# Eight experts taken in the order of their token counts: the three smallest in 64 slots with both halves of the split in one stationary tile, whole-chunk weight splits

## The chip, the cores and the metric

The kernel runs on one core of one Trainium2 chip. The metric is the device time of one execution in microseconds (us). Before the change the median of three runs is 1942.06 us (1941.7 to 1943.23).

## The reference

A trunk of two layers works on 256 tokens of width 1024 in fp32. Each layer has three parallel mixers, a cross-attention and a feed-forward part, each followed by a LayerNorm. The feed-forward part of the first layer is dense; that of the second is a choice of 2 out of 8 experts, and this is the part that the change touches:

```
logits = (x @ w_router).astype(jnp.float32) + b_router.astype(jnp.float32)
top_vals, top_idx = lax.top_k(logits, TOP_K)            # TOP_K = 2
top_w = jax.nn.softmax(top_vals, axis=-1)
combine = jnp.sum(jax.nn.one_hot(top_idx, N_EXPERTS) * top_w[..., None], axis=-2)
out = jnp.zeros_like(x)
for e in range(N_EXPERTS):                              # 8 experts, 1024 -> 2 x 3584 -> 1024
    out = out + combine[..., e:e + 1] * swiglu(x, w_gu[e], w_down[e])
```

With the reference's inputs its routing sends 53, 76, 79, 38, 77, 57, 63 and 69 tokens to experts 0 to 7.

## The kernel before

**Split products.** Every matrix product keeps fp32 accuracy with three products of a shorter type: a tensor w is split into `hi` (ScalarE copies it into the shorter type, `hi_of`) and `lo` (VectorE subtracts, `lo_of`), and a product is hi·hi + hi·lo + lo·hi. Weights arrive in chunks of 128 x 2048 fp32 (1 MB), one DMA each from the SyncE queue, in the order in which they are used. `parts` (line 260) splits a chunk in two halves of 128 x 1024 as they are asked for; the halves of `hi` and of `lo` each live in a ring of three buffers (`wsp`), so that one and a half chunks can stand ready ahead of TensorE. ScalarE writes `whi`, VectorE reads `raw` and `whi` and writes `wlo`, and a chunk's raw buffer is free for the next DMA when VectorE has read its second half.

**Raw buffers.** In the last layer, from the cross-attention on, raw chunks go round a ring of 15 buffers: NFX = 11, one in `xp`, and three in `fifo`.

**The experts (`moe`, line 1170).** After the last LayerNorm the router's logits are turned, VectorE ranks them, and TensorE counts the tokens ahead of each token, which gives each token its slot in each of its two experts (`slot`). `prepare` (1253) builds for a pair of experts a 0/1 matrix `pe` from the slots, gathers by matmul up to 128 tokens per expert (32 matmuls of 256 columns) and copies the result to `xg`, hi and lo apart. Each expert then has 42 chunks. `gate_up` (1292) handles one block of 512 hidden columns: 4 chunks, 48 matmuls of 512 columns with the tokens as the stationary operand (line 1301 hi·hi, 1302 hi·lo, 1303 lo·hi), then SiLU on ScalarE, a product on VectorE, 4 transposes on TensorE (1309), and the split of the result (`hth`, `htl`). `down` (1317) handles 2 chunks, 24 matmuls (lines 450 to 452 of `mm3_x`), one block later than `gate_up`. There are NEB = 7 blocks. `scatter` (1329) splits the sum (`myh`, `myl`), brings it back to token order by 8 matmuls, and adds it to the output with 4 VectorE instructions (line 1340). The experts run in the order 0 to 7. `prepare` stands ahead of expert 0, and at the end of experts 1, 3 and 5 for the next pair.

**More than 128 tokens.** The largest count is read into a register at the end (line 1393); if it is over 128, a loop over all experts does the rest.

**Order.** The order on each engine is made by a scheduler that hoists later work into gaps; the first splits of expert 0's weights thus stand inside the last LayerNorm.

## Time and profile before

| | |
|---|---|
| median of three runs | 1942.06 us |
| the profiled execution: its time | 1947.3 us |
| the profiled execution: span of its core | 1945.4 us |
| mean granted TensorE clock | 0.984 |
| TensorE matmul busy | 1882.1 us (97%) |
| VectorE busy | 1532.6 us (79%) |
| ScalarE busy | 1283.2 us (66%) |
| GpSimd busy | 110.9 us (6%) |
| HBM read | 498.34 MB |

The span runs from the first to the last instruction of the core. Shares of busy time are means over stages that differ: layer 0, the mixer and cross-attention of layer 1 (to about 940 us), and the experts (from there to 1930 us). TensorE's matmuls overlap, and their ends are modelled, so that its busy time is an upper bound of what it does. The groups of the section on the rows are named by number in the prediction.

### The profile page before, as it was taken

Reading aid. Unit: us, or ns where it says so; the run is one execution under the profiler, and the core shown is the slowest. Engines: PE = TensorE matmul, PEld = TensorE weight load, DVE = VectorE, ACT = ScalarE, POOL = GpSimd, SP = SyncE. Lnnn points to the kernel's source line nnn. Section 1 sums busy time; section 2 is a strip of 40 time slices with the busy share of each in tenths; the row PEclk is TensorE's granted clock in tenths of the full one; section 3 lists DMA queues with packets and bytes.
Section 4 is the critical chain, followed back from the end, with each engine's and each line's share of the span. In section 5 each row is a group of like instructions: output and inputs, shape, how many; then the busy total and the mean of one; then the engine's idle time right before and its main releaser. Section 6 shows DMA issues by size and latency. Waiting matters only on the chain.

```text
span 1945.4 us, 27894 instructions
## 1 busy us (share of the span) xinstructions
PE 1882.1 (97%) x10672; PEld 1634.6 (84%) x10672; DVE 1532.6 (79%) x1976; ACT 1283.2 (66%) x1673; POOL 110.9 (6%) x111
## 2 busy tenths in 40 slices
PE   7999999999999999989899999999999999999996
PEld 7998998899989988877688888888888888888875
DVE  7774764794557755755899999999999999999987
ACT  5666554555444555544678787887777778788774
POOL 4030000100004300000200000000000000000000
PEclk9999999999999999989899999999999999999998
DMA  7324553544554343594499998999989999899970
GB/s 255 131 93 153 185 216 134 182 171 163 185 188 170 130 145 121 194 378 173 174 371 371 359 373 320 375 373 355 375 318 375 375 354 374 318 375 368 382 274 24
DMA packets 74924, 503.37 MB, mean 259 GB/s; under 512 B 9504, under 2 KB 11808, under 8 KB 15264
## 3 DMA queue, kind: packets, MB, share of 16 engines
q1 hardware_dynamic: 74496, 500.43, 68.6%
q8 instruction: 85, 1.39, 0.3%
q0 software_dynamic: 144, 1.05, 0.2%
q14 instruction: 55, 0.45, 0.1%
q10 hardware_dynamic: 144, 0.05, 0.0%
HBM read 498.34 MB, written 1.05 MB: 257 GB/s over the span
## 4 chain that ended last, share of the span: by engine, by line
PE 87%; DVE 8%; ACT 3%; issue 2%; DMA 0%; POOL 0%; ACTq 0%; DVEq 0%; POOLq 0%
PE ps L281 8%; PE ps L283 8%; PE ps L282 8%; PE pu L1302 5%; PE dn L450 5%; PE pu L1303 5%; PE pu L1301 5%; PE pg L1303 5%; PE pg L1302 5%; PE dn L451 5%; PE dn L452 5%; PE pg L1301 5%; DVE wlo L221 3%; PE acc L428 2%; PE acc L430 2%; PE acc L432 2%
## 5 line engine op out<-in xcount | busy, mean ns | idle before, releaser
L221 DVE TENSOR_TENSOR wlo<-raw,whi 128x1024 fp32r<-128x1024 f32 x926 | 1118.3, 1229 | 308.4 <-ACT whi L218 295.3
L218 ACT ACTIVATE whi<-raw 128x1024 fp32r<-128x1024 f32 x926 | 974.4, 1060 | 519.3 <-PE ps L282 187.5
L281 PE MATMUL ps<-xhi,whi 128*128 128x256 f32 x992 | 288.3, 291 | 14.8 <-ACT whi L218 14.8
L283 PE MATMUL ps<-xhi,wlo 128*128 128x256 f32 x992 | 286.4, 290 | 4.3 <-DVE wlo L221 4.3
L282 PE MATMUL ps<-xlo,whi 128*128 128x256 f32 x992 | 286.8, 289 | 0.0
L281 PEld LDWEIGHTS ps<-xhi,whi 128*128 128x128 f32 x992 | 194.8, 197 | 16.3 <-ACT whi L218 15.5
L283 PEld LDWEIGHTS ps<-xhi,wlo 128*128 128x128 f32 x992 | 194.8, 197 | 5.8 <-DVE wlo L221 5.1
L282 PEld LDWEIGHTS ps<-xlo,whi 128*128 128x128 f32 x992 | 195.3, 197 | 0.8 <-issue 0.3
L1302 PE MATMUL pu<-wlo,xg 128*128 128x512 f32 x448 | 176.1, 393 | 2.7 <-DVE wlo L221 2.7
L451 PE MATMUL dn<-wlo,hth 128*128 128x512 f32 x448 | 178.0, 400 | 0.1
L1302 PE MATMUL pg<-wlo,xg 128*128 128x512 f32 x448 | 176.6, 394 | 1.4 <-DVE wlo L221 1.4
L1303 PE MATMUL pg<-whi,xg 128*128 128x512 f32 x448 | 175.8, 392 | 0.6 <-DVE xg L1254 0.6
L1301 PE MATMUL pg<-whi,xg 128*128 128x512 f32 x448 | 175.2, 391 | 0.0
L1301 PE MATMUL pu<-whi,xg 128*128 128x512 f32 x448 | 175.1, 391 | 0.0
L1303 PE MATMUL pu<-whi,xg 128*128 128x512 f32 x448 | 174.8, 390 | 0.0
L452 PE MATMUL dn<-whi,htl 128*128 128x512 f32 x448 | 174.0, 391 | 0.0
L450 PE MATMUL dn<-whi,hth 128*128 128x512 f32 x448 | 139.5, 391 | 0.0
L1302 PEld LDWEIGHTS pu<-wlo,xg 128*128 128x128 f32 x448 | 84.1, 188 | 27.6 <-DVE wlo L221 6.6
L1302 PEld LDWEIGHTS pg<-wlo,xg 128*128 128x128 f32 x448 | 84.1, 188 | 24.1 <-DVE wlo L221 3.8
L1301 PEld LDWEIGHTS pu<-whi,xg 128*128 128x128 f32 x448 | 84.1, 188 | 17.9
L450 PEld LDWEIGHTS dn<-whi,hth 128*128 128x128 f32 x448 | 83.9, 188 | 17.8
L1301 PEld LDWEIGHTS pg<-whi,xg 128*128 128x128 f32 x448 | 84.2, 188 | 17.4
(520 smaller groups left out, 2869.5 us busy)
## 6 DMA issues: line engine op xcount, KB each, us to landing
raw<-in_w SPq DMA_DIRECT2D x462, 1024.0 KB, 4.9
lng<-in_ln SPq DMA_DIRECT2D x6, 512.0 KB, 6.4
lnb<-in_ln SPq DMA_DIRECT2D x6, 512.0 KB, 7.2
raw<-in_memt SPq DMA_DIRECT2D x2, 1024.0 KB, 4.7
raw<-in_xt SPq DMA_DIRECT2D x4, 256.0 KB, 5.7
raw<-in_w SPq DMA_DIRECT2D x2, 512.0 KB, 6.0
ux<-us SPq DMA_DIRECT2D x32, 32.0 KB, 2.1
yg<-ux SPq DMA_DIRECT2D x32, 32.0 KB, 1.9
```

The costliest lines, as they stand in the source:

```text
L218: return A.activation(dst, src, AF.Copy, scale=scale)
L221: return V.tensor_sub(dst, src, hi.bitcast(F32))
L281: T.matmul(ps, whi, xhi, start=first, stop=False)
L282: T.matmul(ps, whi, xlo, start=False, stop=False)
L283: return T.matmul(ps, wlo, xhi, start=False, stop=last)
L428: T.matmul(accs[m][n], ah, wh, start=first, stop=False)
L450: T.matmul(ps, ah, wh, start=first, stop=False)
L451: T.matmul(ps, ah, wl, start=False, stop=False)
L452: return T.matmul(ps, al, wh, start=False, stop=last)
L1301: T.matmul(ps, xg[0][:, k, :], wh, start=(k == 0), stop=False)
L1302: T.matmul(ps, xg[0][:, k, :], wl, start=False, stop=False)
L1303: T.matmul(ps, xg[1][:, k, :], wh, start=False, stop=(k == KD - 1))
```

## The change

- **Order by count.** `sort`, on VectorE after the weights of the mixture are known, counts the tokens of experts 1 to 7, ranks them from the largest to the smallest, permutes their slots and weights (`slots`, `combs`), and writes the index of each one's first weight chunk as integers (`firsti`). SyncE reads these seven numbers into registers and takes the weight chunks of experts by register address. Expert 0 runs first as before; then follow, by rank, 0, 4, 1, 5, 2, 6, 3 (`turns`).
- **Three small experts.** Ranks 4, 5 and 6 have 64 slots (HCAP) in place of 128. Their stationary tile holds the hi part in columns 0 to 63 and the lo part in columns 64 to 127, so that two products (with `whi` and with `wlo`) do the work of three: 32 + 16 matmuls per block in place of 48 + 24. The sums of the two halves of the partitions are added behind it: ScalarE copies partitions 64 to 127 of `pg` and `pu` (line 1370), VectorE adds them (1371), then SiLU, product, transposes of 64 partitions, and both splits into one `hth`.
- **Whole-chunk splits.** In the experts `parts` splits a chunk by one ScalarE and one VectorE instruction of 128 x 2048. `hi` goes to a ring of three in `wsp`, `lo` to a new ring of three (`wlo`). Ahead of the experts, halves of `hi` and `lo` share one buffer of `wsp`.
- **Room.** NFX goes from 11 to 8: 12 raw buffers in place of 15.
- **prepare** takes one expert ahead of expert 0, one after the fourth block of expert 0, and pairs at the end of turns 1, 3 and 5: five in place of four.
- The loop for overflow runs if an expert has more tokens than its slots (128, or 64 for the three small ones).

```diff
@@ parts
+            if wide[0]:
+                if not made:
+                    hi = wsp.tile([P, CH], F32R, tag="w", name="whi")
+                    lo = wide[0].tile([P, CH], F32R, name="wlo")
+                    hi_of(hi, raw)
+                    low(lo, raw, hi)
+                    made[0] = hi, lo
+                return [t[:, c0:c1] for t in made[0]]
             h = c0 // HC
             if h not in made:
-                hi = wsp.tile([P, HC], F32R, tag="whi", name="whi")
-                lo = wsp.tile([P, HC], F32R, tag="wlo", name="wlo")
+                both = wsp.tile([P, 2, HC], F32R, tag="w", name="w")
+                hi, lo = both[:, 0], both[:, 1]
...
@@ moe: sort
+                V.tensor_tensor(gt7, others, mine, op=ALU.is_gt)
...
+                V.tensor_reduce(pos7, gt7, axis=AX.X, op=ALU.add)
+                V.tensor_tensor(perm, iota[:, 0:NS].unsqueeze(2).to_broadcast(sh7),
+                                pos7.unsqueeze(1).to_broadcast(sh7), op=ALU.is_equal)
...
+                V.tensor_copy(firsti, first)
...
@@ gate_up
                             T.matmul(ps, xg[0][:, k, :], wh, start=(k == 0), stop=False)
-                            T.matmul(ps, xg[0][:, k, :], wl, start=False, stop=False)
-                            T.matmul(ps, xg[1][:, k, :], wh, start=False, stop=(k == KD - 1))
+                            T.matmul(ps, xg[0][:, k, :], wl, start=False, stop=(few and k == KD - 1))
+                            if not few:
+                                T.matmul(ps, xg[1][:, k, :], wh, start=False, stop=(k == KD - 1))
+                n = HCAP if few else P
...
+                if few:
+                    up = wk.tile([P, 512], F32, tag="htl", name="mup", bufs=2)
+                    for ps, s_ in ((pg, sl), (pu, up)):
+                        A.copy(s_[:n], ps[n:])
+                        V.tensor_add(s_[:n], s_[:n], ps[:n])
+                    A.activation(sl[:n], sl[:n], AF.Silu)
+                    V.tensor_mul(sl[:n], sl[:n], up[:n])
...
@@ the experts
-            for e in range(E):
+            def src(r, off):
+                if r < 0:
+                    return w_in[base + off]
+                if r not in begin:
+                    begin[r] = nc.values_load(firsti[0:1, r:r + 1], engines=[mybir.EngineType.SP], min_val=NCE,
+                                              max_val=NS * NCE)
+                return w_in[ds(begin[r] + (base + off), 1)].rearrange("o p c -> (o p) c")
+
+            turns = [-1, 0, 4, 1, 5, 2, 6, 3]
+            for i, r in enumerate(turns):
...
+                    if i == 0 and nb == 3:
+                        ready += prepare([False], lambda m, j: slots[:, m, turns[1]:turns[1] + 1])
+                if 0 < i < E - 1 and not ready:
+                    rs = turns[i + 1:i + 3]
+                    ready = prepare([q >= NBIG for q in rs], lambda m, j: slots[:, m, rs[j]:rs[j] + 1])
```

The order of the instructions moves at three places. On VectorE, inside the last LayerNorm, before (`bnb` is the shift of the second half of the tokens, `lnx` three of the eight pieces of the normed input to the router):

```order
L238 BN_AGGR bmv<-bst 128x2
L238 TENSOR_SCALAR bve<-bmv 128x1
L238 SCALAR_TENSOR_TENSOR bnb<-bmv,brs 128x1
L221 TENSOR_TENSOR wlo<-raw,whi 128x1024 x3
L238 TENSOR_TENSOR x<-lny,lng 128x1024
L238 TENSOR_SCALAR lnx<-pt,lnt 128x256 x3
L238 TENSOR_TENSOR x<-x,lnb 128x1024
```

and now:

```order
L242 BN_AGGR bmv<-bst 128x2
L242 TENSOR_SCALAR bve<-bmv 128x1
L242 SCALAR_TENSOR_TENSOR bnb<-bmv,brs 128x1
L224 TENSOR_TENSOR wlo<-raw,whi 128x2048 x3
L242 TENSOR_TENSOR x<-lny,lng 128x1024
L242 TENSOR_SCALAR lnx<-pt,lnt 128x256 x3
L242 TENSOR_TENSOR x<-x,lnb 128x1024
```

Three splits stand at the same place, each of a whole chunk in place of a half. On VectorE in the steady part of an expert, before (one block of 6 chunks is the twelve splits from one `htl` to the next):

```order
L221 TENSOR_TENSOR wlo<-raw,whi 128x1024 x6
L1306 TENSOR_TENSOR msl<-msl,pu 128x512
L221 TENSOR_TENSOR wlo<-raw,whi 128x1024 x3
L221 TENSOR_TENSOR htl<-ps,hth 128x512
L221 TENSOR_TENSOR wlo<-raw,whi 128x1024 x9
```

and now one block of a small expert:

```order
L1371 TENSOR_TENSOR msl<-msl,pg 64x512
L224 TENSOR_TENSOR wlo<-raw,whi 128x2048 x2
L1371 TENSOR_TENSOR mup<-mup,pu 64x512
L224 TENSOR_TENSOR wlo<-raw,whi 128x2048
L1373 TENSOR_TENSOR msl<-msl,mup 64x512
L224 TENSOR_TENSOR wlo<-raw,whi 128x2048 x3
L224 TENSOR_TENSOR hth<-ps,hth 128x4x64
```

Twelve splits of halves have become six of whole chunks, and two instructions behind the matmuls four. On the SyncE queue, where the last LayerNorm's loads (`lnb`) are behind it and the experts' chunks follow, before:

```order
L314 DMA lnb<-in_ln 128x1024
L256 DMA raw<-in_w 128x2048 x7
L1393 TENSOR_LOAD cnti
L1393 ISA x2
L256 DMA raw<-in_w 128x2048 x286
```

and now, from the last load of `firsti` on:

```order
L1432 TENSOR_LOAD firsti
L1432 ISA x2
L260 DMA raw<-in_w 128x2048 x2
L1480 TENSOR_LOAD cnti
L1480 ISA x2
L260 DMA raw<-in_w 128x2048 x23
L260 ISA
L260 DMA raw<-in_w 128x2048
```

Seven loads of `firsti` stand in the queue behind those 7 DMAs, with one DMA between the fourth and the fifth, and each chunk taken by register address has one register instruction ahead of it.

## Rows read from the trace of the kernel before

**Rows 1.** Page, part 5: costliest group of TensorE ahead of the experts, with its waits.

```profile
L281 PE MATMUL ps<-xhi,whi 128*128 128x256 f32 x992 | 288.3, 291 | 14.8 <-ACT whi L218 14.8
```

**Rows 2.** Windows: length, PE, PEld, DVE, ACT, POOL busy; clock, DMA share, GB/s.

```profile
830.00:840.00 10.00, 5.45 (x22) 4.86 (x23) 8.36 (x8) 3.06 (x3) 0.00 (x0) 0.54 1.01 427
1200.00:1300.00 100.00, 100.00 (x452) 82.16 (x451) 92.93 (x87) 79.11 (x83) 0.00 (x0) 1.00 0.95 363
```

**Rows 3.** Chain of waits in the experts: start, us, what.

```profile
1070.31 1.40 DVE x L1340 x2
...
1807.30 1.41 DVE x L1340 x2
```

**Rows 4.** Groups by form, 960 to 1910 us: busy us, mean ns of one, idle before.

```profile
L221 DVE TENSOR_TENSOR wlo<-raw,whi 128x1024 fp32r<-128x1024 f32 x653 | 780.8, 1223 | 69.9 <-ACT whi L218 57.9
L218 ACT ACTIVATE whi<-raw 128x1024 fp32r<-128x1024 f32 x651 | 684.5, 1060 | 194.0 <-PE pu L1303 68.0 <-PE pg L1303 67.6 <-PE dn L452 53.6
L221 DVE TENSOR_TENSOR htl<-ps,hth 128x512 fp32r<-128x512 f32 x55 | 37.7, 686 | 1.7 <-ACT hth L218 1.7
L218 ACT ACTIVATE hth<-ps 128x512 fp32r<-128x512 f32 x55 | 32.0, 581 | 4.8 <-PE ps L1309 4.8
L1254 DVE CAST xg<-ps 128x256 fp32r<-128x256 f32 x24 | 10.0, 419 | 0.5 <-PE ps L1273 0.5
```

**Rows 5.** Timeline of VectorE in an expert: start, us.

```profile
1300.91 0.68 DVE L1306 TENSOR_TENSOR msl<-msl,pu 128x512 f32<-128x512 f32 x1
1301.58 3.50 DVE L221 TENSOR_TENSOR wlo<-raw,whi 128x1024 fp32r<-128x1024 f32 x3
...
1312.50 1.28 DVE L221 TENSOR_TENSOR myl<-dn,myh 128x512 fp32r<-128x512 f32 x2
```

**Rows 6.** Chain of waits: steps of TensorE.

```profile
906.72 0.91 PE acc L428 x4
...
1847.92 0.45 PE ps L1309 x4
```

**Rows 7.** Timeline of TensorE at a `prepare` between experts.

```profile
1186.19 0.64 PE L1273 MATMUL ps<-pe,xhi 128*128 128x256 f32 x4
1186.66 0.63 PE L450 MATMUL dn<-whi,hth 128*128 128x512 f32 x2
```

**Rows 8.** Timelines of VectorE, GpSimd and ScalarE in the last LayerNorm.

```profile
925.72 5.64 DVE L221 TENSOR_TENSOR wlo<-raw,whi 128x1024 fp32r<-128x1024 f32 x3
932.42 0.98 DVE L238 TENSOR_SCALAR lnx<-pt,lnt 128x256 f32<-128x256 f32 x2
936.44 0.28 DVE L238 TENSOR_TENSOR cmp<-lg 128x128 f32<-128x128 f32 x1
939.61 0.87 DVE L238 TENSOR_SCALAR pe<-cr,slot 128x128 fp32r<-128x128 f32 x4
...
925.86 3.29 POOL L238 TENSOR_TENSOR x<-x,lnb 128x1024 f32<-128x1024 f32 x1
```

**Rows 9.** Chain of waits: TensorE's first `prepare`.

```profile
940.43 4.39 PE ps L1273 x24
```

**Rows 10.** SyncE: waits, 960 to 1880 us (us, times, longest), and one register load.

```profile
SPq L256 <- DVE wlo L221: 772.5, 309, 4.6
...
L1393 SPq TENSOR_LOAD <-cnti x1: 488/488/488, 957.6 to 957.6; - x1
```

**Rows 11.** Windows of 2 us around falls and rises of the granted clock.

```profile
726.00:728.00 2.00, 2.00 (x12) 2.00 (x11) 1.56 (x2) 0.52 (x2) 0.00 (x0) 0.50 0.03 8
728.00:730.00 2.00, 2.00 (x17) 1.86 (x15) 0.18 (x1) 1.20 (x3) 0.00 (x0) 0.92 0.77 180
...
932.00:934.00 2.00, 1.12 (x5) 0.19 (x4) 1.76 (x4) 0.00 (x0) 0.10 (x1) 1.00 0.93 393
934.00:936.00 2.00, 0.94 (x5) 0.29 (x4) 1.64 (x3) 0.64 (x1) 0.00 (x0) 1.00 0.14 57
936.00:938.00 2.00, 0.16 (x1) 0.16 (x1) 1.84 (x8) 1.36 (x2) 0.00 (x0) 0.63 0.00 0
```

More of the change, by code (lines that the diff above doesn't have):

```diff
@@ L39 @@
 NCE = 42
+HCAP = 64
+NBIG = 4
 ALPHA = (2.0 * L) ** 0.25
@@ L42 @@
 NFIFO = 3
-NFX = 11
+NFX = 8
 LATER = 400
@@ L93, in _constants @@
     e = np.arange(E)
+    put("half", np.tile(i % HCAP, (P, 1)))
     put("lt", np.tile((e[None, :] < e[:, None]).astype(np.float32).reshape(1, 64), (P, 1)))
@@ L227, in tile_trunk @@
     load = [None]
+    wide = [None]
     class Line:
@@ L1243, in weigh, with sort @@
                 V.tensor_add(comb, comb, tmp8)
+                GP.tensor_scalar(x, x, ALPHA, None, op0=ALU.mult)
+            NS = E - 1
+            sh7 = [P, NS, NS]
+            sq = [P, 2, NS, NS]
+            slots, combs, over = t("slots", [P, 2, NS]), t("combs", [P, 2, NS]), t("over", [P, E])
+            capn, firsti = t("capn", [P, E]), mp.tile([P, NS], I32, name="firsti")
+            def sort():
                 ps = pst.tile([P, 512], F32, tag="tr", name="ps")
@@ new lines, in sort @@
+                gt7, eq7 = (old[:, o:o + NS * NS].rearrange("p (e f) -> p e f", e=NS) for o in (0, NS * NS))
+                pos7, perm = t("pos7", [P, NS]), t("perm", sh7)
+                first, most = t("first", [P, NS]), t("most", [P, 1])
+                others = cnt[:, 1:].unsqueeze(1).to_broadcast(sh7)
+                mine = cnt[:, 1:].unsqueeze(2).to_broadcast(sh7)
+                lt7 = ltm[:, 1:, 1:]
+                V.tensor_tensor(gt7, others, mine, op=ALU.is_gt)
+                V.tensor_tensor(eq7, others, mine, op=ALU.is_equal)
@@ new lines, in sort @@
+                V.tensor_copy(firsti, first)
+                both = old2[:, 0:2 * NS * NS].rearrange("p (m e f) -> p m e f", m=2, e=NS)
+                for dst, src in ((slots, slot), (combs, comb)):
+                    V.tensor_mul(both, perm.unsqueeze(1).to_broadcast(sq),
+                                 src[:, :, 1:].unsqueeze(2).to_broadcast(sq))
+                    V.tensor_reduce(dst, both, axis=AX.X, op=ALU.add)
+                V.memset(capn, -float(P))
+                V.tensor_scalar(capn[:, 1:], pos7, float(NBIG) - 0.5, float(P - HCAP), op0=ALU.is_gt, op1=ALU.mult)
@@ L1254, in prepare @@
+                V.tensor_scalar(capn[:, 1:], capn[:, 1:], -float(P), None, op0=ALU.add)
+                V.tensor_add(over, cnt, capn)
+                V.tensor_reduce(most, over, axis=AX.X, op=ALU.max)
+                V.tensor_scalar(most, most, 0.0, None, op0=ALU.max)
+                V.tensor_copy(cnti, most)
+            def prepare(few, slot_col, dv=None):
                 dv = dv or (lambda f, *a, **k: f(*a, **k))
+                ne = len(few)
                 pe = wk.tile([P, 2, ne, P], F32R, tag="pe", name="pe", bufs=1)
@@ L1257, in prepare @@
                     for m in range(2):
-                        dv(V.tensor_scalar, pe[:, m, e, :], iota, 1.0, slot_col(m, e), op0=ALU.add, op1=ALU.is_equal)
+                        dv(V.tensor_scalar, pe[:, m, e, :], R("half") if few[e] else iota, 1.0, slot_col(m, e),
+                           op0=ALU.add, op1=ALU.is_equal)
                 if isinstance(dv, Line):
                     dv(lo_of, xn_lo[:, 0], x[:, 0], xn_hi[:, 0])
-                xg = [[wk.tile([P, KD, P], F32R, tag=f"xg{i}", name=f"xg{i}", bufs=2) for i in range(2)]
+                xg = [[wk.tile([P, KD, P], F32R, tag=f"xg{i}", name=f"xg{i}", bufs=2) for i in range(2 - few[e])]
                       for e in range(ne)]
@@ L1292, in gate_up @@
             def gate_up(xg, src):
+                few = len(xg) == 1
                 pg = psg.tile([P, 512], F32, tag="gu", name="pg")
@@ L1325, in down @@
                         wh, wl = w(kk * D + n * 512, kk * D + (n + 1) * 512)
-                        mm3_x(pd[n], ht[0][:, j, :], ht[1][:, j, :], wh, wl, nb == 0 and j == 0,
-                              nb == NEB - 1 and j == 3)
+                        first, last = nb == 0 and j == 0, nb == NEB - 1 and j == 3
+                        if len(ht) == 1:
+                            T.matmul(pd[n], ht[0][:, j, :], wh, start=first, stop=False)
+                            T.matmul(pd[n], ht[0][:, j, :], wl, start=False, stop=last)
+                        else:
+                            mm3_x(pd[n], ht[0][:, j, :], ht[1][:, j, :], wh, wl, first, last)
             def scatter(pd, pet, cw):
@@ L1342, in moe @@
             base = pos[0]
-            def gsrc(e, nb):
-                return lambda c: w_in[base + NCE * e + 4 * nb + c]
-            def dsrc(e, nb):
-                return lambda c: w_in[base + NCE * e + 4 * NEB + 2 * nb + c]
-            ready = prepare(2, lambda m, e: slot[:, m, e:e + 1], dv)
+            wide[0] = es.enter_context(tc.tile_pool(name="wlo", bufs=3, reuse_waits="tile"))
+            ready = prepare([0], lambda m, e: slot[:, m, 0:1], dv)
             with tc.issue_after(dv.prev.ins):
                 weigh()
-            for e in range(E):
+                sort()
+            begin = {}
+            def src(r, off):
[7 more added lines that the diff above has]
+            for i, r in enumerate(turns):
                 xg, pet = ready.pop(0)
```

80 lines of the change are left out of this document (44 added, 36 removed).

## The prediction

> **What bounds the kernel now.** I read the windows first, then the chain of waits, then the groups by form, then the timelines of VectorE and TensorE. In the experts (940 to 1930 us, half of the span) every resource is nearly full: in one window of 100 us TensorE is busy all the time at full clock, VectorE 92.9 us, ScalarE 79.1 us, the DMA engines 0.95 [rows 2]. Which of them sets the pace is read from the chain: it runs along TensorE, and the adds of one scatter in every second expert come 245.66 us apart, (1807.30 - 1070.31) / 3 [rows 3]. TensorE's own work gives nearly that: a matmul of 512 columns every 0.2275 us (0.91 for 4) and a transpose every 0.11 us [rows 6], so 42 chunks x 12 x 0.2275 = 114.7, 28 transposes 3.2, 8 matmuls of scatter 1.8: 119.7 us for an expert; a `prepare` is 32 matmuls at 0.47 / 4 us [rows 7] and four transposes, 4.2. A pair is 243.6 us, and 2.1 are stalls. VectorE waits for ScalarE, which waits for TensorE to free split buffers [rows 4]; SyncE waits for VectorE's splits to free raw buffers [rows 10]. **TensorE is the bound, and VectorE is 7% behind it.** What a third fewer matmuls in three experts is worth therefore depends on VectorE.
>
> **VectorE's price in an expert.** Back to back, three splits of a half take 3.50 us, so one starts every (3.50 - 1.22) / 2 = 1.14 us [rows 5]. Its cost per column is (1223 - 686) / 512 = 1.05 ns [rows 4]; a whole chunk then starts every 1.14 + 1.07 = 2.21 us, in place of 2.28 for two halves. The wide split saves VectorE only 42 x 0.07 = 3 us per expert. Instructions of 512 columns start every 0.60 (`myl`, 1.28 for two of 0.68) to 0.67 us (`msl` to the next split) [rows 5]: 0.65. One of 256 columns lasts 0.42 [rows 4]: 0.37. I assume that 64 partitions cost as much as 128, as time goes by columns here; no row shows it.
>
> A big expert asks VectorE for 42 x 2.21 + 7 x 2 x 0.65 + scatter (2 x 0.65 + 2.8 for four adds, rows 3) + 2 = 108 us, below TensorE's 119.7: it stays bound by TensorE, and VectorE ends it with its three buffers ahead. **A small expert** costs TensorE 42 x 8 x 0.2275 = 76.4 plus about 4, some 80 us, but VectorE per block 6 x 2.21 + 3 x 0.65 + 0.37 = 15.6, 7 x 15.6 = 109 us ahead of scatter. It becomes bound by VectorE, and 40 us that TensorE saves shrink to about 10.
>
> **A small expert and the big one behind it**, from TensorE's start on the small one:
> - VectorE is 2 to 3 chunks ahead (a ring of 3); I take 2.5. It has 39.5 chunks left, and TensorE stays on its heels until the sixth chunk of the big expert, where both scatters are done: 45.5 x 2.21 = 100.6.
> - Seven times two adds, a product and a split: 7 x (3 x 0.65 + 0.37) = 16.2.
> - The adds of the scatter before, 2.8, and the small expert's own scatter, 4.1: 6.9. What is left of `prepare` (four copies of 128 columns, four `pe` for 0.87 [rows 8]): 1.9. One product of the big expert: 0.65. Sum 126.3.
> - TensorE then has the rest: 119.7 + 4.2 of `prepare` - 5 chunks x 2.73 = 110.3.
> - Together 236.6 against 245.66: 9.1 less, and **27.2 in three such pairs**. With a lead of 2 or 3 chunks and 0.60 to 0.69 for 512 columns this is 20 to 35.
>
> **The other parts.**
> - *Last LayerNorm.* Three splits stand ahead of VectorE's `x` and `lnx`, on the chain. They took 5.64 us, beside a GpSimd instruction of 3.29 us [rows 8]; three alone took 3.50 [rows 5]. Whole chunks add 3 x 1.07: **+3.2** (0 if the transposes were late anyway, 5 if GpSimd slows them again).
> - *First prepare.* Two `pe` in place of four, -0.4 [rows 8]. 32 gathers of 128 columns in place of 256, which came every 4.39 / 24 = 0.18 us [rows 9]: between nothing and half of 5.9; I take -1. Together **-1.4**.
> - *One more prepare*, in expert 0: 32 matmuls of 128 columns and two transposes on the bounding engine. At the price of 256 columns 4.0, by columns 2.1 (no row shows 128): **+3**.
> - *sort*: 22 VectorE instructions of at most 128 columns, 0.2 to 0.3 us each [rows 8], about 5.5 us, between the splits of the first chunks. Cover: three whole chunks (8.2 us of TensorE's work) are split ahead, before only one and a half. **+1**, at worst 5.5.
> - *SyncE.* The seven loads wait for `firsti`, and every DMA behind them waits too, then 7 x 0.49 us [rows 10]. Chunks in the ring cover that. Register addresses add an instruction to each DMA of a queue that waited 772.5 us for buffers [rows 10]: 0.
> - *DMA, and 12 raw buffers for 15.* A small expert takes a chunk every 15.6 / 6 = 2.6 us, 403 GB/s. The queue gave 427 when it was full, and 363 at a share of 0.95 when it was not [rows 2]. If 363 / 0.95 = 382 were all, a chunk would take 2.74 us and a small expert would use up 42 x 0.14 = 6 us, or 2 of the 12 chunks, which the next big one gives back: 0.
> - *ScalarE*: by (1060 - 581) / 512 = 0.94 ns per column [rows 4] a whole chunk lasts 1.06 + 0.96 = 2.02 us, a small block 6 x 2.02 + 4 others of at most 0.58 = 14.4, below 15.6: no bound, if it isn't late (a rival).
> - *Shared buffer ahead of the experts*: `hi` is freed a matmul later, about 0.12 us. TensorE waited 14.8 us for `whi` in its largest group [rows 1]; 0, at worst a few us.
> - *Stalls in the first two big experts* (2.1 in a pair) fall with a deeper lead: **-1**.
>
> **Sum**: -27.2 + 3.2 - 1.4 + 3 + 1 - 1 = -22.4 on the profiled execution (1947.3 us, span 1945.4). That is 5.2 above the median of 1942.06; I take the difference over to the median: about **1919 us**.
>
> **Row and rule.** Between two splits of a half lie 1.14 us though one lasts 1.22 [rows 5]: the end of one overlaps the start of the next. The Trainium skill, VectorE: DVE Perf Modes, section on the DRAIN that cannot be avoided, says that the next instruction does not start until the pipe is empty. By the row's spacing the sum stands as above; by the full duration it is the fourth rival's. The page's errata section has fp32 tensor_tensor at (N + 151) / 0.96 GHz, 2.29 us for 2048 columns, against 1.22 + 1.07 = 2.29 from rows here, so that only the spacing is in dispute.
>
> **Rivals.**
> 1. *Waits in the small block (slower).* VectorE's add of `mup` waits for ScalarE's copy of `pu`, which waits for TensorE's last matmul of the block and stands in ScalarE's queue behind whole-chunk splits; all splits behind the add wait too, and TensorE for them. For it: after the last chunk TensorE needs 1.8 us, a split of ScalarE 2.02, the copy 0.58, sum 4.4, and only two splits of VectorE, 4.4, stand between the adds. Against it: that just fits, and ScalarE is rarely late now (57.9 us in 950, rows 4). If one ScalarE split is missed per block: 21 x 2.02 = +42, **1961**. It decides from 22.4 / 21 = 1.1 us per block.
> 2. *The clock falls.* In a small expert TensorE works 1.8 of every 2.6 us and then waits. For it: with 0.16 busy of 2 us the clock was on its way from 2.4 to 1.2 GHz. Against it: with 1.12 and 0.94 of 2 us it stayed at 2.4, and a busy TensorE at 1.2 got 2.4 back [rows 11]. At 1.2 GHz a block takes 48 x 0.455 + 0.4 = 22.2, an expert 159, 46 more than VectorE's; half the time so in three experts gives +69, **1988**. It decides from a sixth of the time. [...]
> 3. *VectorE isn't the bound*: splits overlap with other work better than rows 5 show. Then a pair is 80 + 123.9 = 203.9, three save 125, and the time is about **1822**. Against it: VectorE's sum is taken from its busiest stretches.
> 4. *An instruction of VectorE takes its whole duration*: 45.5 x 0.08 + 26 x 0.04 = 4.7 more per pair, 14 in all, **1933**.
> 5. *The change doesn't apply*: the three small experts hold 63, 57 and 38 tokens by the reference's routing; were one over 64, all eight would run again, 4 x 245.66 = 983 us more, **about 2900**. 63 of 64 is close, but the routing would have to differ by two tokens.
>
> **How the numbers follow.** Forecast 0.71, rivals 1 to 5: 0.11, 0.06, 0.03, 0.08, 0.01. The forecast's own bounds: a lead of 3, 0.60 us, and the cheap ends at the start give 1900; a lead of 2, 0.67 us, sort and LayerNorm at their dear ends give 1940. The range 1900 to 1944 takes in rival 4 and the mild end of rival 1; outside stay some 0.06 below and 0.14 above. 0.2% (3.9 us) is what a measurement can tell from no change: faster 0.79 (nearly all of the forecast, 3 and 4, a bit of 1), same 0.08 (the edges of 1 and 4), slower 0.13.
>
> **What the new profile would show.** Right: in the small experts VectorE over 95% busy, TensorE 70 to 75% at full clock, waiting for `wlo`; about 111 us for each; big ones near 120; `wlo` of 2048 columns 2.29 us each, 2.21 apart; the three splits in the LayerNorm 8 to 9 us. Wrong: VectorE idle there behind ScalarE's `mup` or `msl` (rival 1), a granted clock below 1 (rival 2), small experts of 85 us (rival 3), or SyncE the last releaser of TensorE's waits.

## The result, and the profile after

The changed kernel takes 1991.88 us (median of 4 runs, 1991.41 to 1996.83) against 1942.16 (four runs of the kernel before): 1.0262 times as long, 95% interval 1.0247 to 1.0277. Forecast was 1919, in a range of 1900 to 1944. The change is slower by 50 us, and the prediction was wrong by 73.

In the profiled execution the span grew from 1945.4 to 1990.4 us. Four places make up the 45.0: up to the last LayerNorm it is 5.0 us shorter (its first instruction starts at 911.32 in place of 916.28), which need not be the change's doing, since the profiled execution of before lies 5.2 us above its median; from there to the first gate matmul it takes 34.6 us in place of 28.4, +6.2; from there to the first expert's first add 140.2 in place of 125.7, +14.5; and from that add to the last expert's first add 887.7 in place of 858.7, +29.0. What follows the last add is as long as before.

| | before | after |
|---|---|---|
| span of the profiled execution | 1945.4 us | 1990.4 us |
| mean granted TensorE clock | 0.984 | 0.965 |
| TensorE matmul busy | 1882.1 us (97%) | 1837.1 us (92%) |
| VectorE busy | 1532.6 us (79%) | 1510.1 us (76%) |
| ScalarE busy | 1283.2 us (66%) | 1238.2 us (62%) |

TensorE, VectorE and ScalarE have less to do than before and the span is longer: what was added is waiting. VectorE's splits, as a group by form from 960 to 1975 us [rows 4], wait longer for ScalarE's, 114.5 us in place of 57.9, and last 2.285 us each:

```profile
L224 DVE TENSOR_TENSOR wlo<-raw,whi 128x2048 fp32r<-128x2048 f32 x331 | 752.5, 2285 | 115.8 <-ACT whi L221 114.5
```

The adds of every expert on VectorE's timeline (start, us), which answer to [rows 3]; expert 0 comes first, and the small ones are third, fifth and seventh:

```profile
1086.05 1.40 DVE L1417 SCALAR_TENSOR_TENSOR x<-ps,comb,x 128x512 f32<-128x512 f32 x2
1230.35 0.74 DVE L1417 SCALAR_TENSOR_TENSOR x<-ps,combs,x 128x512 f32<-128x512 f32 x1
1347.13 1.40 DVE L1417 SCALAR_TENSOR_TENSOR x<-ps,combs,x 128x512 f32<-128x512 f32 x2
1487.12 1.39 DVE L1417 SCALAR_TENSOR_TENSOR x<-ps,combs,x 128x512 f32<-128x512 f32 x2
1603.36 1.40 DVE L1417 SCALAR_TENSOR_TENSOR x<-ps,combs,x 128x512 f32<-128x512 f32 x2
...
1973.79 0.75 DVE L1417 SCALAR_TENSOR_TENSOR x<-ps,combs,x 128x512 f32<-128x512 f32 x1 [0.77 <-PE ps L1416]
```

A small expert takes 116.8 and 116.2 us from add to add (111 were forecast), a big one that ends with a `prepare` 144.3 and 140.0. In the kernel before it was 129.3 with a `prepare` and 116.4 without. So a pair takes 256 to 261 us; 236.6 were forecast, 245.66 it was.

Windows of the changed kernel, a big expert's middle, a small one's, and 30 us at the end of the first sorted big expert (columns as in [rows 2]):

```profile
1120.00:1180.00 60.00, 60.00 (x267) 48.49 (x266) 51.86 (x29) 43.14 (x29) 0.00 (x0) 1.00 0.98 370
1260.00:1320.00 60.00, 50.77 (x202) 33.99 (x201) 60.00 (x40) 52.07 (x40) 0.00 (x0) 1.00 1.00 405
1190.00:1200.00 10.00, 7.17 (x33) 5.67 (x32) 7.71 (x6) 4.74 (x5) 0.00 (x0) 0.88 1.00 387
1200.00:1210.00 10.00, 8.58 (x35) 6.62 (x34) 4.54 (x7) 5.45 (x6) 0.00 (x0) 0.78 0.36 127
1210.00:1220.00 10.00, 7.60 (x25) 6.09 (x26) 2.88 (x5) 3.15 (x4) 0.00 (x0) 0.66 0.42 159
```

The middles are as forecast: TensorE is busy all the time in the big expert, VectorE in the small one, both at full clock. At the end of the expert nothing is full: TensorE waits, its granted clock falls to 0.66, VectorE is busy 2.9 us of 10, and the DMA share drops to 0.36. TensorE's timeline there shows on what it waits:

```profile
1188.49 0.40 PE L466 MATMUL dn<-wlo,hth 128*128 128x512 f32 x1
...
1190.12 0.40 PE L467 MATMUL dn<-whi,htl 128*128 128x512 f32 x1
...
1193.16 0.60 PE L1379 MATMUL ps<-cst,msl 128*128 128x128 f32 x4
...
1195.81 0.50 PE L465 MATMUL dn<-whi,hth 128*128 128x512 f32 x1 [1.58 <-ACT hth L221]
...
1198.25 1.22 PE L1331 MATMUL ps<-pe,xhi 128*128 128x256 f32 x4 [1.25 <-DVE htl L224]
...
1212.40 0.80 PE L1361 MATMUL pg<-whi,xg 128*128 128x512 f32 x1 [3.05 <-DVE xg L1310]
1212.99 0.63 PE L1362 MATMUL pg<-wlo,xg 128*128 128x512 f32 x1
...
1217.26 0.63 PE L1362 MATMUL pg<-wlo,xg 128*128 128x512 f32 x1
```

and ScalarE's and VectorE's what stood ahead of `hth` and `htl` in their queues:

```profile
1193.36 1.92 ACT L221 ACTIVATE whi<-raw 128x2048 fp32r<-128x2048 f32 x1 [0.88 <-PE dn L467]
1195.17 0.58 ACT L221 ACTIVATE hth<-ps 128x512 fp32r<-128x512 f32 x1
...
1217.50 3.72 ACT L221 ACTIVATE whi<-raw 128x2048 fp32r<-128x2048 f32 x2 [4.47 <-PE pg L1361]
```

```profile
1189.12 0.68 DVE L1376 TENSOR_TENSOR msl<-msl,pu 128x512 f32<-128x512 f32 x1
...
1195.30 2.29 DVE L224 TENSOR_TENSOR wlo<-raw,whi 128x2048 fp32r<-128x2048 f32 x1 [0.50 <-ACT whi L221]
1197.51 0.68 DVE L224 TENSOR_TENSOR htl<-ps,hth 128x512 fp32r<-128x512 f32 x1
...
1209.85 2.29 DVE L224 TENSOR_TENSOR wlo<-raw,whi 128x2048 fp32r<-128x2048 f32 x1 [0.83 <-ACT whi L221]
1212.06 0.48 DVE L1310 CAST xg<-ps 128x128 fp32r<-128x128 f32 x2
```

The last block's hidden tile has no next block to hide behind. Its product `msl` is done at 1189.8, the transposes follow at 1193.16 only, behind all 24 matmuls of the block ahead, and `hth` and `htl` each stand behind a whole-chunk split of the next expert's weights. So does the last of the `prepare` copies (`xg` at 1212.06), for which TensorE waits 3.05 us. The waits then feed on themselves: from 1212.99 to 1217.26 ten steps of TensorE take 0.427 us each at the lower clock (1.2 GHz), where 0.233 is usual, and ScalarE's splits wait 4.47 us until TensorE has freed their buffers. TensorE's first two rows show something else: from 1188.49 to 1190.12 matmuls start 0.233 us apart (seven steps), where it was 0.2275 [rows 6].

In the last LayerNorm and the first `prepare` (VectorE, the second and third split also by themselves; GpSimd; then the chain), the rows that answer to [rows 8, 9]:

```profile
918.63 11.01 DVE L224 TENSOR_TENSOR wlo<-raw,whi 128x2048 fp32r<-128x2048 f32 x3
920.84 4.45 DVE L224 TENSOR_TENSOR wlo<-raw,whi 128x2048 fp32r<-128x2048 f32 x1
925.21 4.43 DVE L224 TENSOR_TENSOR wlo<-raw,whi 128x2048 fp32r<-128x2048 f32 x1
...
919.92 3.21 POOL L242 TENSOR_TENSOR x<-lny,lng 128x1024 f32<-128x1024 f32 x1 [1.41 <-ACT lny L242]
923.22 4.27 POOL L242 TENSOR_TENSOR x<-x,lnb 128x1024 f32<-128x1024 f32 x1
```

```profile
939.01 7.06 PE ps L1331 x32
```

The three splits take 11.01 us in place of 5.64. Ahead of the first gate matmul stand 32 gathers of 128 columns in 7.06 us, where 24 of 256 columns took 4.39. The granted clock differs there; windows of the changed kernel (the first), and of the kernel before:

```profile
939.00:946.00 7.00, 6.99 (x33) 7.00 (x34) 1.89 (x3) 1.17 (x2) 5.39 (x1) 0.50 0.00 1
```

```profile
940.40:942.30 1.90, 1.87 (x9) 1.90 (x10) 1.22 (x2) 0.00 (x0) 0.59 (x1) 0.50 0.06 13
943.30:944.30 1.00, 1.00 (x11) 1.00 (x9) 0.77 (x2) 0.74 (x3) 1.00 (x1) 0.98 0.00 0
```

At 0.50 gathers of either width start 0.21 us apart; the changed kernel has all 32 of them there, the kernel before 13, and the others 0.12 apart at full clock.

### The profile page after: what moved, and what is told of

The parts are those of the page before. It is cut to its first block, busy times and chain, and to the rows that moved or that the text cites. A ratio compares the mean times of both kernels' runs of the same rounds, so it can differ in the third digit from the quotient of the medians.

```text
span 1990.4 us, 26609 instructions
## 1 busy us (share of the span) xinstructions
PE 1837.1 (92%) x10200; PEld 1554.0 (78%) x10200; DVE 1510.1 (76%) x1698; ACT 1238.2 (62%) x1373; POOL 115.5 (6%) x111
## 4 chain that ended last, share of the span: by engine, by line
PE 76%; DVE 12%; issue 3%; DMA 3%; ACT 3%; POOL 2%; DVEq 0%; SPq 0%; POOLq 0%; ACTq 0%
DVE wlo L224 8%; PE ps L298 8%; PE ps L296 8%; PE ps L297 8%; PE pg L1362 5%; PE pg L1361 4%; PE pu L1361 4%; PE pu L1362 3%; PE pg L1364 3%; PE dn L467 3%; PE pu L1364 3%; DMA raw<-in_w 3%; PE dn L465 3%; PE dn L466 3%; PE acc L445 2%
## 5 line engine op out<-in xcount | busy, mean ns | idle before, releaser
L224 DVE TENSOR_TENSOR wlo<-raw,whi 128x2048 fp32r<-128x2048 f32 x336 | 768.1, 2298 | 116.0 <-ACT whi L221 114.7
L221 ACT ACTIVATE whi<-raw 128x2048 fp32r<-128x2048 f32 x336 | 641.9, 1916 | 220.9 <-PE dn L467 64.7
L224 DVE TENSOR_TENSOR w<-raw,w 128x1024 fp32r<-128x1024 f32 x254 | 315.0, 1243 | 220.7 <-ACT w L221 217.5
L221 ACT ACTIVATE w<-raw 128x1024 fp32r<-128x1024 f32 x254 | 267.7, 1058 | 157.6 <-PE acc L447 60.1
L296 PE MATMUL ps<-xhi,w 128*128 128x256 f32 x992 | 287.3, 290 | 13.4 <-ACT w L221 13.4
L298 PE MATMUL ps<-xhi,w 128*128 128x256 f32 x992 | 285.1, 288 | 5.5 <-DVE w L224 5.5
L297 PE MATMUL ps<-xlo,w 128*128 128x256 f32 x992 | 284.8, 288 | 0.0
L296 PEld LDWEIGHTS ps<-xhi,w 128*128 128x128 f32 x992 | 193.5, 195 | 15.1 <-ACT w L221 13.9
L298 PEld LDWEIGHTS ps<-xhi,w 128*128 128x128 f32 x992 | 193.3, 195 | 7.2 <-DVE w L224 6.5
L297 PEld LDWEIGHTS ps<-xlo,w 128*128 128x128 f32 x992 | 194.0, 196 | 0.6 <-issue 0.2
L466 PE MATMUL dn<-wlo,hth 128*128 128x512 f32 x280 | 110.9, 398 | 0.0
L467 PE MATMUL dn<-whi,htl 128*128 128x512 f32 x280 | 110.3, 400 | 0.0
```

What stands on the lines that cost most here:

```text
L221: return A.activation(dst, src, AF.Copy, scale=scale)
L224: return V.tensor_sub(dst, src, hi.bitcast(F32))
L296: T.matmul(ps, whi, xhi, start=first, stop=False)
L297: T.matmul(ps, whi, xlo, start=False, stop=False)
L298: return T.matmul(ps, wlo, xhi, start=False, stop=last)
L466: T.matmul(ps, ah, wl, start=False, stop=False)
```

## The experiments

The theory after the first comparison: whole-chunk splits lengthen what stands ahead of the hidden tile and of the `prepare` copies at an expert's end. Rivals: the small experts and 12 raw buffers; sort, register addresses and the extra `prepare`. Each result is a ratio to the kernel before, run on the same chip. "Add to add" is the time from one expert's first add to the next one's.

**One part alone, or one part undone.** Wide splits on the kernel before (the new `parts`, NFX = 8):

```diff
+            wide[0] = es.enter_context(tc.tile_pool(name="wlo", bufs=3, reuse_waits="tile"))
             base = pos[0]
```

> The kernel before with one part of the change: splits of a whole chunk in the experts (three buffers of each part, 12 raw buffers). No sort, no small experts. Theory (a whole-chunk split in the in-order queues of VectorE and ScalarE holds up the last block and the prepare of every second expert; 16 to 20 us for each of three, 4 in the LayerNorm): 1990 to 2005 us, the adds of every second expert about 262 us apart in place of 245.7. Rival B (the small experts and the twelve raw buffers starve the splits): 1942 to 1955. Rival C (sort, register addresses and the extra prepare): 1942 to 1950.

Measured 2005.27 us, 1.0316 (1.0295 to 1.0337): the whole loss and more, with neither sort nor small experts. But add to add is 135.8 with a `prepare` (129.3 before) and 127.0 without one (116.4): the end of every expert got longer, so that the `prepare` isn't the heart of it. Next, all experts in 128 slots:

```diff
-NBIG = 4
+NBIG = 7
```

> The changed kernel with 128 slots for every expert (NBIG 7): wide splits, sort and register addresses stay, no small experts. Theory: 2005 to 2020 us, as the wide splits alone plus some 14 for the prepare in the first expert. Rival B (the small experts are what costs): 1945 to 1960. Rival C (sort, registers, extra prepare): 1990 or more, with the wide splits alone at 1945.

2009.46 us, 1.0348 (1.0325 to 1.0372): 4 us more than the wide splits alone, with sort, register addresses and one `prepare` added; both rivals fall. The spacing of the matmuls also goes from 0.2320 to 0.2333 here (see "The address"), 8 x 504 x 0.0013 = 5 us, so that the 4 us can't be put down to sort and `prepare`. Then the other way round, everything but the wide splits:

```diff
-            wide[0] = es.enter_context(tc.tile_pool(name="wlo", bufs=3, reuse_waits="tile"))
```

> The changed kernel with splits of half a chunk (three buffers of half a chunk, both parts in one), sort and small experts kept, 12 raw buffers. Theory: a big expert with a prepare at its end falls from 140 to about 124 us, a small one rises from 116.5 to about 120: 1935 to 1955 us. Rival B: 1985 to 1995, big ones still near 140. Rival C: 1980 to 1990.

1947.27 us, 1.0017 (1.0003 to 1.0030). Undoing the wide splits takes back 45 us. The theory's size for the small experts was off: 112 to 113 us, not 120. Width was parted from depth with six buffers of a half, the same room as three of a chunk:

```diff
-                both = wsp.tile([P, 2, HC], F32R, tag="w", name="w")
+                if wide[0] and turn[0] % 2:
+                    both = wide[0].tile([P, 2, HC], F32R, name="w")
+                else:
+                    both = wsp.tile([P, 2, HC], F32R, tag="w", name="w")
+                turn[0] += 1
...
```

> The changed kernel with splits of half a chunk in six buffers, which hold as much as the three of a whole chunk: width without depth changed. Theory: if the width alone holds up the queues, a big expert with a prepare takes about 123 us, a small one 117: 1925 to 1945 us. If it is the depth (splits issued further ahead of the last block's own work), 1975 to 1995, near the changed kernel. Rival B: 1980 to 1995.

1957.10 us, 1.0077 (1.0056 to 1.0098), between the two cases: twice the depth costs 10 us, twice the width about 35. A deeper ring lets more splits into the queue ahead of the hidden tile: at the end of the first sorted big expert five splits of a half stand on VectorE between `msl` (1182.73) and `htl` (1189.72), three with the ring of three (1182.53 to 1186.72), and TensorE waits 0.72 us for `hth`, where it did not. The rooms themselves are cheap:

```diff
-NFX = 11
+NFX = 8
```

> The kernel before with 12 raw buffers in place of 15 and nothing else. In the wide-only kernel a matmul of a big expert came every 0.232 us, in the changed kernel and the one with halves every 0.233, in the kernel before every 0.2275. Rival D1 (fewer raw buffers, or the addresses that go with them, lengthen the spacing): 0.232 to 0.234 here, eight experts x 504 x 0.0055 = 22 us, 1955 to 1965. Theory (the splits' buffers do it, or nothing in the memory): spacing 0.2275, 1941 to 1947.

1947.63 us, 1.0023 (1.0011 to 1.0035), spacing 0.2277: 4 us, and not the spacing. One buffer for both parts:

```diff
-                hi = wsp.tile([P, HC], F32R, tag="whi", name="whi")
-                lo = wsp.tile([P, HC], F32R, tag="wlo", name="wlo")
+                both = wsp.tile([P, 2, HC], F32R, tag="w", name="w")
+                hi, lo = both[:, 0], both[:, 1]
```

> The kernel before with both parts of a half in one buffer (three of them) in place of a ring for each part; 15 raw buffers. Rival D2 (the shared buffer, freed for both parts at once, lengthens the spacing of the matmuls): 0.232 to 0.234, 1955 to 1965. Theory: 0.2275, 1940 to 1946.

1943.77 us, 1.0002 (0.9990 to 1.0014): nothing. And the changed kernel with the kernel before's buffers (halves, a ring for each part, NFX = 11):

> The changed kernel with splits of a half in a ring for each part and 15 raw buffers, as in the kernel before; sort and small experts stay. Theory (everything that the wide splits and their memory cost is undone; what is left is the small experts, bound by VectorE at 112 us against 116.4, and the extra prepare): with a spacing of 0.2275 1930 to 1938 us; with 0.233 as in the kernel with halves and 12 buffers 1943 to 1948.

1947.30 us, 1.0024 (1.0011 to 1.0037), spacing 0.233. So neither raw buffers nor rings bring the spacing back.

**The end of an expert.** `turned[0]` is the last transpose of the block; in an expert's last block the second chunk of `down` is put behind it:

```diff
-                    for kk, n in kn:
...
+                    with tc.issue_after(turned[0].ins) if last_block and c == 1 else ExitStack():
+                        for kk, n in kn:
...
```

> The changed kernel with one thing moved: in the last block of an expert the four transposes of the hidden tile stand on TensorE ahead of the second of the two chunks that follow, not behind both, so that ScalarE's and VectorE's splits of the hidden tile come some 2.8 us earlier, ahead of the next whole-chunk splits. Theory (at an expert's end the hidden tile waits behind whole-chunk splits in the queues, TensorE waits for it and its clock falls): 3 to 6 us less for each of five big experts, 1962 to 1977. Rival (the prepare's copies are what holds the queues, the transposes don't matter): 1987 to 1995.

1973.94 us, 1.0149 (1.0131 to 1.0166): 18 us less by the place of four small instructions. TensorE, ScalarE and VectorE at the same end of expert:

```profile
1186.24 0.60 PE L1381 MATMUL ps<-cst,msl 128*128 128x128 f32 x4
...
1191.35 0.74 PE L1331 MATMUL ps<-pe,xhi 128*128 128x256 f32 x4 [0.30 <-DVE htl L224]
...
1202.01 2.08 PE L1331 MATMUL ps<-pe,xlo 128*128 128x256 f32 x8 [4.33 <-DVE xg L1310]
```

```profile
1188.27 0.58 ACT L221 ACTIVATE hth<-ps 128x512 fp32r<-128x512 f32 x1
1189.68 1.92 ACT L221 ACTIVATE whi<-raw 128x2048 fp32r<-128x2048 f32 x1 [0.83 <-PE dn L467]
```

```profile
1185.01 0.68 DVE L1378 TENSOR_TENSOR msl<-msl,pu 128x512 f32<-128x512 f32 x1
...
1190.61 0.69 DVE L224 TENSOR_TENSOR htl<-ps,hth 128x512 fp32r<-128x512 f32 x1
```

`hth` now stands ahead of the split that it stood behind, and `htl` starts 5.6 us after `msl` in place of 8.4; the waits of 1.58 and 1.25 us are 0.30 together. What the rival named is there too: TensorE still waits 4.33 us at a stretch for the `prepare` copies. The same edit in the kernel before, where splits are half as long:

> The kernel before with the transposes of an expert's last block early and nothing else: how much of the gain of the kernel with halves, padding and early transposes (1935) is owed to the sort and the small experts. If all of it is: 1940 to 1945. If the early transposes give it: 1932 to 1938.

1945.83 us, 0.9997 (0.9985 to 1.0009): there the wait is hidden already.

**The address.** Every kernel with the sort had matmuls 0.233 us apart in big experts, with any kind of split. The sort's small tensors lie ahead of the experts' work buffers and move them: the stationary tiles (`xg`, `hth`, `htl`) begin at multiples of 1024 bytes, before at 480 or 1504 above a multiple of 2048 (addresses in the built programs). In the kernel with halves and 15 raw buffers:

```diff
+            t("pad", [P, 120])
```

> The kernel with halves and 15 raw buffers, with 480 bytes of padding ahead of the experts' work buffers and nothing else. There the stationary tiles begin at addresses that are multiples of 1024 bytes; in the kernel before at 480 and 1504 above a multiple of 2048, now at 1504. Rival D3 (that address sets the spacing of the matmuls): 0.2275 us again in place of 0.2339, 5 x 504 x 0.006 + 3 x 336 x 0.006 = up to 20 us less, 1925 to 1935. Theory without it: spacing 0.2335, 1944 to 1950.

1936.40 us, 0.9967 (0.9952 to 0.9982), spacing 0.2275. In the kernel before with 12 raw buffers, `t("pad", [P, 136])` puts them onto multiples of 1024:

> The kernel before with 12 raw buffers (1947.6, spacing 0.2277) and padding that puts the stationary tiles on multiples of 1024 bytes, as the change did. If the address sets the spacing: 0.2335, 8 x 504 x 0.0058 = 23 us more, 1962 to 1972. If it was something else that the padding of the kernel with halves touched: 1945 to 1950.

1969.86 us, 1.0137 (1.0120 to 1.0155): 22 us more, by an unused tile of 544 bytes. Matmuls of one big expert, the 12-buffer kernel without the padding:

```profile
1009.72 0.39 PE L1302 MATMUL pg<-wlo,xg 128*128 128x512 f32 x1
...
1014.70 0.39 PE L1301 MATMUL pu<-whi,xg 128*128 128x512 f32 x1
```

and with it:

```profile
1009.67 0.40 PE L1303 MATMUL pg<-wlo,xg 128*128 128x512 f32 x1
...
1015.97 0.40 PE L1303 MATMUL pu<-wlo,xg 128*128 128x512 f32 x1
```

22 steps in 4.98 us are 0.2264 each, 27 in 6.30 are 0.2333; from 980 to 1060 us the means are 0.2277 and 0.2332. The padding is the only difference of the two sources. Then the changed kernel with 480 bytes:

> The changed kernel with the same 480 bytes of padding and nothing else (whole-chunk splits, small experts). If the address of the stationary tiles sets the spacing here too: 0.2275 us in place of 0.2333, some 10 to 20 us less, 1972 to 1982. If with whole-chunk splits it stays between the two, as in the wide-only kernel (0.232 with stationary tiles at 480 above a multiple of 2048): 1982 to 1988. If the address matters only with splits of a half: 1988 to 1995.

1984.20 us, 1.0209 (1.0191 to 1.0226): 8 us less, but the spacing stays at 0.232. With whole-chunk splits something else holds it up, as in the wide-only kernel (0.232 with the old addresses); what, was not found. Both repairs together:

> The changed kernel with the padding and the transposes of the last block early. If the two costs stand beside each other: 1974 less what the padding alone saves, 1955 to 1968. What is then left above the kernel with halves and padding (1936) is the price of whole-chunk splits in the LayerNorm (4), and of the prepares and the small experts behind splits twice as long.

1968.98 us, 1.0131 (1.0114 to 1.0148). 8 and 18 would give 1966: they nearly add up. The same two with halves:

> The kernel with halves, 15 raw buffers and padding (1936), with the transposes of the last block early. Theory (the hidden tile waits behind splits at an expert's end, half as long as with whole chunks): 1 to 2 us less for each of five big experts, 1926 to 1932. Rival (with halves the wait is hidden already): 1934 to 1938.

1935.04 us, 0.9957 (0.9946 to 0.9968), 1 us from the kernel without the early transposes: the rival holds. Against 1969 the difference of 34 us is the whole-chunk splits with their deeper ring and 12 raw buffers (4 us by themselves, above), after the two repairs. Most of it shows from add to add: the three big experts with a `prepare` at their end take 134.5, 134.1 and 133.6 us with whole chunks and 128.1, 126.5 and 126.5 with halves, the small ones 117.8, 118.0 and 118.8 against 113.0, 113.9 and 114.4. Some 2 us of each big one is the spacing (0.232 against 0.2275). TensorE and VectorE at the first of these ends, with whole chunks:

```profile
1200.64 2.08 PE L1332 MATMUL ps<-pe,xlo 128*128 128x256 f32 x8 [4.34 <-DVE xg L1311]
```

```profile
1197.97 2.28 DVE L224 TENSOR_TENSOR wlo<-raw,whi 128x2048 fp32r<-128x2048 f32 x1
1200.17 0.74 DVE L1311 CAST xg<-ps 128x256 fp32r<-128x256 f32 x2
```

The `prepare` copy stands behind a whole-chunk split, and TensorE waits 4.34 us for it; with halves its waits for these copies there are 0.42 and 0.27 us. No run moves these copies by themselves, so that their share of the 34 us is not shown.

**What the small experts are worth.** Two ways to fill the idle time of each engine with the other kind of expert. First a small one's chunks in turn with a big one's:

```diff
+            groups = [[-1], [0, 4], [1, 5], [2, 6], [3]]
...
+            def run(left):
+                while left:
+                    go = []
+                    for x_ in left:
+                        s_ = next(x_, "over")
...
```

> As the one before, with a small expert's chunks taken in turn with those of the big one ahead of it (three pairs; first and last big expert alone; one PSUM buffer moved from the gates to the sums, 14 raw buffers, no prepare in the middle of the first expert). A pair then asks TensorE for 119.7 + 80 + 8 = 208 us, VectorE for 84 x 2.28 + 9 + 16 + 8 + 3 = 228, the DMA queue for 84 MB at about 400 GB/s, 220. Theory (VectorE's time is lost only because it idles in big experts behind TensorE and TensorE in small ones behind it): a pair 230 to 235 us in place of 243.6, the kernel 1900 to 1915. Rival (VectorE and the DMA queue are full in the small experts only, so that the pair stays at the sum of the two): 1935 to 1950.

1949.94 us, 1.0036 (1.0023 to 1.0048): the theory missed by 35 us and more. In the middle of a pair both VectorE and the DMA queue are nearly full (1150 to 1290), but at the pair's beginning nothing is full:

```profile
1090.00:1110.00 20.00, 13.43 (x39) 8.54 (x40) 12.67 (x13) 10.25 (x13) 0.00 (x0) 0.76 0.73 292
1150.00:1290.00 140.00, 133.75 (x554) 97.07 (x552) 135.27 (x131) 116.30 (x131) 0.00 (x0) 1.00 0.99 388
```

Then two lanes that end at different times (14 raw buffers here too):

```diff
+            big, few = lane([-1, 0, 1, 2, 3], ready[0], True), lane([4, 5, 6], None, False)
```

> Splits of a half as in the kernel with halves and 15 raw buffers, and two lanes: the five big experts one after the other, and the three small ones beside them, a block of a small one between a big block's gates and the sums before it, two for every three big blocks. Ends and prepares of one lane then lie beside the other lane's work. VectorE is asked for 336 x 2.28 + 5 x 9 + 3 x 16 + 8 x 4.1 = 892 us, the DMA queue at 390 GB/s for 903, TensorE for 5 x 119.7 + 3 x 80 + 8 x 4 = 870. Theory (the pairs' ends cost the interleaved kernel its gain): experts in 905 to 940 us in place of 984, the kernel 1870 to 1905. Rival (queues kept in order lock up between two lanes as well): 1930 to 1955.

1945.25 us, 1.0005 (0.9995 to 1.0016): a miss by 40 us and more. VectorE is busy 132 of 140 us there and waits for ScalarE; why the lanes don't fill up was not settled. Last, VectorE's own work in a small block. It sums the two half blocks (`mup`, `msl`); TensorE can do this while it turns them, with `fold` (two unit matrices, one above the other) as the moving tile:

```diff
-                    for ps, s_ in ((pg, sl), (pu, up)):
-                        A.copy(s_[:n], ps[n:])
-                        V.tensor_add(s_[:n], s_[:n], ps[:n])
...
+                    for i, (p_, s_) in enumerate(((pg, sl), (pu, up))):
+                        A.copy(s_, p_)
+                        for j in range(4):
+                            turned[0] = T.matmul(ps[:, i, j], s_[:, j * P:(j + 1) * P], fold, start=True, stop=True)
...
```

> The kernel with halves, padding and early transposes (1935), with the sum of a small expert's two half blocks taken from VectorE: ScalarE copies both gates out, TensorE sums the halves while it turns them (8 matmuls of 64 columns in place of 4 transposes a block), and VectorE is left with a product and a split of 256 columns, about 0.8 us a block in place of 2.4. Theory (a small expert of 113 to 114 us is bound by VectorE, 111.97 of 113.1 us busy): 7 x 1.6 = 11 us less work, then bound by the DMA queue at 108 to 110; three of them, 9 to 18 us less, 1917 to 1926. Rival (the DMA queue, at a share of 0.96 there, is the bound already): 1932 to 1937.

1922.51 us, 0.9879 (0.9860 to 0.9898), in the theory's range and faster than both kernels. One small expert, from add to add, without it and with it:

```profile
1204.10:1317.20 113.10, 99.88 (x373) 60.55 (x373) 111.97 (x118) 97.05 (x112) 0.00 (x0) 1.00 0.96 374
```

```profile
1206.10:1313.60 107.50, 101.22 (x456) 74.59 (x456) 102.35 (x103) 93.14 (x112) 0.00 (x0) 0.98 0.98 400
```

VectorE falls from 112.0 to 102.4 us and the expert from 113.1 to 107.5; the DMA queue, now at a share of 0.98 and 400 GB/s, has little left. The lanes with padding and this sum:

> The two lanes with both the padding and the sum on TensorE. If VectorE and the spacing of the matmuls held the lanes at 1945: 10 us of VectorE's 33 on the path and 10 of spacing, 1920 to 1930. If the order of the queues at the ends of blocks holds them: 1938 to 1947.

1935.68 us, 0.9945 (0.9925 to 0.9964): between the two cases: the sum and the spacing were a part of what holds the lanes; that the order of the queues is the rest is likely, but not shown.

## Why the prediction was wrong

**What held.** TensorE bounds a big expert in its middle and VectorE a small one, by the windows above. VectorE's price was right: a block of a small expert was forecast at 15.6 us, and two starts of the same add are 15.34 apart, the 64 partitions of an add costing what 128 do (0.67 us against 0.68):

```profile
1258.16 0.67 DVE L1371 TENSOR_TENSOR msl<-msl,pg 64x512 f32<-64x512 f32 x1
1258.76 4.48 DVE L224 TENSOR_TENSOR wlo<-raw,whi 128x2048 fp32r<-128x2048 f32 x2
...
1266.56 6.68 DVE L224 TENSOR_TENSOR wlo<-raw,whi 128x2048 fp32r<-128x2048 f32 x3
...
1273.50 0.67 DVE L1371 TENSOR_TENSOR msl<-msl,pg 64x512 f32<-64x512 f32 x1
```

Two whole-chunk splits take 4.48, so the second starts 2.2 us after the first, which lasts 2.28. Ends and starts overlap, and rival 4 is out. The Trainium skill, VectorE: DVE Perf Modes, section on the DRAIN that cannot be avoided, has besides the rule that the prediction cites an exception to it: a next instruction that is not held starts earlier. The rows agree with the exception, 2.2 us from start to start against 2.28. Rival 2 is out as well in the place it had: with TensorE busy 50.77 of 60 us the clock stayed at 1.00. Sort and the extra `prepare` were put at 4 us; the kernel with 128 slots is 4 us above the one with wide splits alone, but the spacing makes up as much, so that no run shows the 4.

**The step that failed first**: a big expert "stays bound by TensorE, and VectorE ends it with its three buffers ahead". The sum compared the engines' work over a whole expert and took the stalls between experts (2.1 us a pair) over, as falling with a deeper lead. An expert's end is not a matter of work but of a chain: product, transposes, `hth`, `htl`, last matmuls, then the `prepare` copies, each in a queue with splits ahead of it. Splits twice as long, and three chunks of them ahead in place of one and a half, lengthen each step; TensorE then idles, gets the lower clock (0.66 in the worst window), frees the split buffers later, and the raw chunks stop (a DMA share of 0.36). A big expert with a `prepare` at its end took 139 to 144 us from add to add, and not some 124 (119.7 and a `prepare`). The lead that the prediction counted as a gain is a part of the loss (10 us with six buffers of a half), the length the larger one (about 35). Of the whole loss the place of the transposes is worth 18 us; the copies of the `prepare` behind whole-chunk splits are seen in the trace, but not undone by a run. Rival 1 had the mechanism, an instruction behind whole-chunk splits of an in-order queue, but put it into the small blocks, where it cost nothing, and gave it 0.11.

**The step that failed second**: "42 chunks x 12 x 0.2275 = 114.7" for every expert after the change. The spacing became 0.233, 504 x 0.0055 = 2.8 us for each of five big experts, 14 in all by this sum; mending the address gave back 11 us with halves, and 8 with whole chunks, where the spacing fell to 0.232 only. Nothing in the rows of before could show that; that no price of before need hold for buffers laid elsewhere could have been said.

**Sizes.** The LayerNorm and the first `prepare` together were put at +1.8 and cost 6.2. The splits there cost 5.4, not 3.2. Before, one of GpSimd's two instructions ran among the three splits, and they took 2.1 us more than alone (5.64 against 3.50); now both do, and they take 4.3 more (11.01, against 6.68 in the fence above). The Trainium skill, SBUF — State Buffer, section on the two separate sides, says that VectorE with two SBUF inputs and GpSimd lock each other out of a shared pair of ports for a whole instruction. The trace agrees: the second split ends at 925.29, 2.2 us after GpSimd's first instruction (923.13), GpSimd's second at 927.49, 2.2 after that split, and the third split at 929.64, 2.2 after that; the durations of 3.21 and 4.27 us contain GpSimd's own waits (the first took 2.34 in the kernel before, where it ran ahead of the splits). The gathers were put at -1 for their half width and added 2.7 on the chain (7.06 in place of 4.39): at this clock the width saved nothing (0.21 us apart at either), and TensorE had the lower clock through all of them.

**The gain itself** was forecast at 27 us for three pairs. With the wide splits undone and the address mended, sort and small experts give 8 (the kernel at 1935), far less, since a half-chunk small expert asks VectorE for nearly as much (112 us) as a big one without a `prepare` takes (116.4). The forecast for the split price was thus right and its use wrong: VectorE's 0.07 us per chunk are lost many times over at the ends. With the sums moved off VectorE, small experts give 23 us (the kernel at 1923), near what was forecast, in another way.

## What to carry to other kernels

Wider instructions on an in-order queue raise the latency of everything behind them: besides the work of each engine, write down the longest chain where nothing covers it (the last block, the hand-over to the next stage), and count for each step one instruction of the queue ahead of it. Where a small instruction there feeds the engine that bounds, its place in the order is worth more than cheaper work elsewhere (18 us for four transposes). And after any edit that moves buffers, compare the spacing of unchanged instructions first: a padding of some hundred bytes can undo what looks like a cost of the change.

## What the hardware did that was not expected

- Matmuls of 512 columns with the same data and clock come 0.2277 us apart or 0.2332 (means from 980 to 1060 us), as the work buffers lie 480 and 1504 bytes above a multiple of 2048 or on multiples of 1024; that is 22 us of this kernel. Which of the tiles in those buffers does it was not tried.
- A gather of 128 columns took nearly as long as one of 256 at the same granted clock: both start 0.21 us apart at 0.50, and 0.105 (eight from 1018.03 to 1018.87) against 0.12 at 1.00.
- Three whole-chunk splits took 11.01 us beside two GpSimd instructions, and 6.68 without them: the two engines took turns, a whole instruction each.
